# A list scheduler's clock model rewritten: durations by form of instruction, a port that VectorE and GpSimd share, and convolution taps put into VectorE's gaps

## The chip, the cores and the metric

The kernel runs on one core of a Trainium2 chip. The metric is the time of one execution on the device in microseconds; the time before is the median of three runs. A profile is one more execution of the same program, taken by the hardware profiler.

## The reference

One inference step of two layers, for a prompt of 1024 tokens and for 8 samples of 4 tokens each, which share the weights. The model width is 1024, everything is float32. Cut to what matters here:

```python
def even_layer(x, pos, conv_buf, kv_cache, pre_g, post_g, w_in, w_out, conv_w, conv_b, ln_g, ln_b):
    h = rms_norm(x, pre_g)
    proj = jnp.einsum('ntd,de->nte', h, w_in)                  # 1024 -> 7 * 1024
    a_val, a_gate, a_out_gate, qb, kb, vb, b_gate = jnp.split(proj, [...], axis=-1)
    ya, conv_new = conformer_conv(a_val, a_gate, conv_buf, conv_w, conv_b, ln_g, ln_b)
    ya = ya * jax.nn.silu(a_out_gate)       # GLU, causal depthwise conv of 31 taps, LayerNorm, swish
    q, k, v = rope(qb, pos), rope(kb, pos), vb                 # 16 heads of 64
    parts = [dswa_prompt(q, k, v, wnd, dil) for (wnd, dil) in ((128, 1), (512, 4), (2048, 16))]
    yb = dswa_merge(parts) * jax.nn.silu(b_gate)               # the samples use a cache of 2048 rows
    y = jnp.einsum('nte,ed->ntd', jnp.concatenate([ya, yb], axis=-1), w_out)
    return x + rms_norm(y, post_g), conv_new, k, v

def odd_layer(x, s0, lb, pre_g, post_g, w_in, w_out, g_norm):
    proj = jnp.einsum('ntd,de->nte', rms_norm(x, pre_g), w_in) # 1024 -> 4 * 2048
    qc, fc, ic, gate = jnp.split(proj, [...], axis=-1)
    o, s_new = hgrn2_recurrence(silu(qc), 1 - f, ic, log(f), s0)   # f = lb + (1 - lb) * sigmoid(fc)
    y = jnp.einsum('nte,ed->ntd', rms_norm(o, g_norm) * jax.nn.silu(gate), w_out)
    return x + rms_norm(y, post_g), s_new
```

## The kernel before

All instructions are recorded in one pass by a list scheduler that is part of the kernel. Every engine call goes through `Proxy` (its `g` is line 152, so nearly every row of the profile has that line), which emits the instruction and lets `account` (line 189) advance a model clock `clk` of that engine. The model clocks decide the order of emission; on the chip each engine runs its own instructions in that order and waits on semaphores where data is missing.

The dense work comes in **jobs** (`dense`, `plan_jobs`): 128 output channels of a projection, in three **chunks** of 384, 384 and 288 tokens. Weights and activations are split into a high and a low part, so a chunk is 24 matmuls of 128 rows by 128 columns (three for each of eight k-tiles) which sum in one PSUM bank: one of three banks named `d`, or one of four named `x` when `evacuate`'s queue is longer (`spare` in `dense`). The bank comes free when the job's `evac` has run, mostly a VectorE multiply out of PSUM (`b<-d`), for the rotary q and k also four ScalarE copies of 32 partitions each. `ahead` loads the next weights and splits them: ScalarE casts the high part, `w_split` subtracts it on VectorE or GpSimd, whichever clock is earlier, by a margin (128x1024 elements).

Everything else is **threads** of **atoms**, each with a kind (its engine), a priority and dependencies. After every third matmul of a chunk `sides` looks for an atom whose time has come: a TensorE atom if its data is in by the model 300 ns earlier (`LEAD`), another if it is ready and its engine's clock is at most so far ahead of TensorE's clock. So side work is put between the matmuls of the chunks. `tt` and `copy` choose the engine by the clocks too.

In layer 0 the jobs of a pair of heads come in the order ag, av, v, k, q, and there are eight pairs. Each pair brings two big threads:

- `attention`: for each of eight blocks of 128 queries a step `qk` (scores of two heads into two `x` banks, then on VectorE the mask and the maximum, on ScalarE the exponential), a step `tr` and from the third block on `far` (transposes of the probabilities, copied out of `x`), and a step `pv` (into bank `o`); `tr` of a block stands behind `qk` of the next. At the end `fin1` takes the reciprocal of the denominators on VectorE (128x16) and transposes it on TensorE.
- `conv_thread`: 25 taps on VectorE, each a `scalar_tensor_tensor` of 128x1024, behind one `tensor_scalar`, all in one accumulation; five more taps are made by ScalarE and GpSimd. Its priority number is 5, the last.

Layer 1 has 16 heads with four jobs each and a chunked recurrence; each layer ends with an output projection (`project`) whose last chunk runs through all 16 weights.

Of the kernel before, what the change touches and what calls it, by code (L numbers as in the profile page):

```python
# [12 lines left out]
OP = mybir.AluOpType  # L13
# [34 lines left out]
PTAPS = 5  # L48

# [13 lines left out]
class Arena:  # L63
    SIZE = {"page": 1056, "half": 520, "small": 136}
    BUFS = {"page": 28, "half": 17, "small": 5}
# [23 lines left out]
    def claim(self, o, need):  # L89
        """Sets what o may hold from now on, if that fits beside what the others hold or may still take."""  # L90
# [46 lines left out]
class Thread:  # L137
    def __init__(self, name, prio, atoms, dep=None, done=None):
        self.name, self.prio, self.atoms, self.pos = name, prio, atoms, 0
        self.dep, self.done, self.last = dep, done, 0.0  # L140
        self.owner = Owner()


class Proxy:
# [3 lines left out]
    def __getattr__(self, name):  # L148
        f = getattr(self.real, name)

        def g(*a, **k):
            r = f(*a, **k)  # L152
            self.kern.account(self.eng, name, a)
            return r
# [17 lines left out]
class Kern:  # L172
    def __init__(self, tc, io, arena, psum, dram):
# [5 lines left out]
        self.cur, self.eng, self.end = 0.0, None, 0.0  # L179
        self.xrel, self.drel, self.orel = [0.0] * NX, [0.0] * 3, [0.0]  # L180
# [8 lines left out]
    def account(self, e, name, a):  # L189
# [12 lines left out]
        ps = lambda i: len(a) > i and hasattr(a[i], "space") and a[i].space == bass.MemoryType.PSUM  # L202
        n = free_size(a[0]) if a and hasattr(a[0], "shape") else 0
        if len(a) > 1 and hasattr(a[1], "shape"):
            n = max(n, free_size(a[1])) if e != "pe" else n
        if name.startswith("preload"):
            d = 1283
        elif e == "pe":
            m = 32 if a[0].shape[0] <= 32 else 64 if a[0].shape[0] <= 64 else 128
            if name == "transpose":  # L210
                d = 109
            elif a[1].dtype == F32R:
                d = max(n / 2.4, 0.79 * m) + 3 if m == 128 else n / 2.4 * m / 128 + 25
            else:
                d = (2 * max(n / 1.2, 107) + 4 if m == 128 else n / 0.6 * m / 128 + 23 if m == 32 else
                     max(n / 1.2 + 36, 82))
        elif e == "dve":
            if name == "memset":
                d = 0.53 * n + 69
            elif name == "reciprocal":  # L220
                d = 6 * n + 69
            elif name == "tensor_scalar" and not ps(1):
                d = 0.52 * n + 160
            else:
# [2333 lines left out]
```

## Time and profile before

| | |
|---|---|
| three runs | 2482.09, 2483.13, 2484.84 us; median 2483.13 us |
| span of the profiled execution | 2483.4 us, from its first to its last instruction |
| TensorE busy | 2327.9 us (94%) |
| VectorE busy | 1698.1 us (68%) |
| ScalarE busy | 1080.3 us (44%) |
| GpSimd busy | 1034.0 us (42%) |
| mean granted TensorE clock | 0.971 of full speed |

The profiled execution's own time is its span; its difference to the median of the runs is 0.3 us. "Busy" is the time in which an engine had an instruction in work; for TensorE, whose matmuls overlap, it is not a measure of speed. In layer 0 VectorE is busy nearly all the time, in layer 1 TensorE is.

### The profile page before, as it was taken

How to read it: one execution, taken by the hardware profiler on the slowest of the kernel's cores; microseconds unless marked ns; L12 is line 12 of the kernel's file. 1: busy time of each engine (PE TensorE's matmuls, PEld its weight loads, DVE VectorE, ACT ScalarE, POOL GpSimd, SP SyncE). 2: the span in 40 equal slices, each digit the busy share in tenths (PEclk: the TensorE clock that was granted, in tenths of full speed). 3: DMA queues.
4: the chain of work that ended last, by engine and by line, in shares of the span. 5: the costliest groups of instructions: out<-in, count | busy, mean ns of one | idle time of the engine just before them, and what ended most of it. 6: DMA issues, size and time to landing. Idle time of an engine off the chain costs nothing.

```text
span 2483.4 us, 41427 instructions
## 1 busy us (share of the span) xinstructions
PE 2327.9 (94%) x16619; PEld 2173.2 (88%) x16619; DVE 1698.1 (68%) x2625; ACT 1080.3 (44%) x1972; POOL 1034.0 (42%) x670
## 2 busy tenths in 40 slices
PE   7899899988998989999979999999999999999997
PEld 6887887878878879889969999999999999999997
DVE  8888988978879765654395666666666556667437
ACT  5444535544545432334245444444444444444332
POOL 5553553643645443333262333333333333333334
PEclk9999999999999999999989999999999999999998
DMA  4121221312302687886252111111111221132525
GB/s 151 45 74 37 71 63 38 82 28 69 85 21 98 219 331 274 322 310 230 93 173 91 61 61 61 61 61 61 61 64 62 74 74 61 61 106 95 176 79 188
DMA packets 118168, 271.51 MB, mean 109 GB/s; under 512 B 32336, under 2 KB 59472, under 8 KB 117968
## 3 DMA queue, kind: packets, MB, share of 16 engines
q1 hardware_dynamic: 117968, 268.78, 31.7%
q8 instruction: 133, 2.18, 0.4%
q14 instruction: 67, 0.55, 0.1%
HBM read 215.00 MB, written 53.73 MB: 108 GB/s over the span
## 4 chain that ended last, share of the span: by engine, by line
PE 37%; DVE 14%; ACT 3%; issue 3%; DMA 1%; POOL 1%; SPq 0%; ACTq 0%; POOLq 0%; DVEq 0%
PE d L152 33%; DVE b L152 13%; PE x L152 4%; ACT b L152 3%; POOL b L152 1%; DVE c L152 1%; DMA b<-x1d 1%; DMA b<-vc 0%; DMA b<-woc 0%; POOL c L152 0%; ACT c L152 0%; SPq L152 0%; ACTq L152 0%; POOLq L152 0%; DVE b L2068 0%
## 5 line engine op out<-in xcount | busy, mean ns | idle before, releaser
L152 PE MATMUL d<-c,b 128*128 128x384 f32 (+1 forms) x10512 | 1845.9, 332 | 41.9 <-ACT b L152 29.9
L152 PEld LDWEIGHTS d<-c,b 128*128 128x128 f32 x10512 | 1730.1, 192 | 97.6 <-issue 44.3
L152 POOL TENSOR_TENSOR b<-b,b 128x1024 fp32r<-128x1024 f32 (+7 forms) x404 | 845.1, 2101 | 812.7 <-ACT b L152 557.8
L152 ACT ACTIVATE b<-b 128x384 f32<-128x384 f32 (+14 forms) x647 | 360.8, 567 | 887.8 <-DVE b L152 859.1
L152 DVE SCALAR_TENSOR_TENSOR b<-b,c,b 128x1024 f32<-128x1024 f32 (+2 forms) x258 | 399.4, 1550 | 24.6 <-ACT b L152 21.9
L152 DVE TENSOR_TENSOR b<-b,b 128x384 f32<-128x384 f32 (+15 forms) x411 | 351.2, 863 | 83.1 <-ACT b L152 66.0
L152 DVE TENSOR_TENSOR b<-d,b 128x384 f32<-128x384 f32 (+3 forms) x376 | 192.4, 513 | 281.9 <-PE d L152 280.6
L152 ACT CAST b<-b 128x1024 fp32r<-128x1024 f32 (+5 forms) x408 | 292.8, 724 | 43.8 <-DVE b L152 23.0
L152 PE MATMUL x<-b,b 128*32 128x128 f32 (+10 forms) x3712 | 289.1, 332 | 19.3 <-DVE b L152 13.6
L152 DVE SCALAR_TENSOR_TENSOR b<-b,b 128x384 f32<-128x384 f32 (+3 forms) x216 | 200.6, 933 | 114.6 <-ACT b L152 112.2
L152 PEld LDWEIGHTS x<-b,b 128*32 128x32 f32 (+2 forms) x3712 | 212.9, 138 | 73.4 <-issue 30.8
L152 PE MATMUL x<-c,b 128*128 128x128 f32 (+4 forms) x1024 | 153.5, 285 | 41.9 <-ACT b L152 25.4
L152 PEld LDWEIGHTS x<-c,b 128*128 128x128 f32 (+3 forms) x1024 | 124.4, 144 | 55.7 <-ACT b L152 30.6
L152 ACT COPY b<-d 32x384 f32<-32x384 f32 (+2 forms) x214 | 95.7, 447 | 136.3 <-DVE b L152 92.5
L152 POOL TENSOR_SCALAR b<-b 128x32 f32<-128x32 f32 x40 | 29.3, 733 | 294.0 <-DVE b L152 288.5
L152 DVE COPY b<-x 128x512 f32<-128x512 f32 (+5 forms) x239 | 110.6, 478 | 41.6 <-PE x L152 34.8
L152 POOL COPY b<-b 128x32 f32<-128x32 f32 (+1 forms) x105 | 59.9, 587 | 163.6 <-DVE b L152 161.4
L152 DVE CUSTOM_DVE_ANT_0 b<-x,b 128x256 f32<-128x256 f32 (+8 forms) x144 | 71.7, 535 | 76.3 <-PE x L152 76.3
L152 ACT COPY b<-x 128x512 f32<-128x512 f32 (+5 forms) x145 | 72.7, 512 | 112.7 <-PE x L152 110.1
L152 ACT ACTIVATE b<-b,c 128x512 f32<-128x512 f32 (+1 forms) x112 | 94.3, 872 | 1.9 <-DVE b L152 0.8
L152 POOL TENSOR_TENSOR b<-b,c 128x248 f32<-128x248 f32 (+1 forms) x48 | 59.3, 1252 | 72.1 <-ACT b L152 47.8
L152 DVE TENSOR_SCALAR b<-b,b 128x128 f32<-128x128 f32 x112 | 79.0, 705 | 4.0
(58 smaller groups left out, 926.9 us busy)
## 6 DMA issues: line engine op xcount, KB each, us to landing
b<-wc SPq DMA_DIRECT2D x64, 512.0 KB, 4.8
b<-wab SPq DMA_DIRECT2D x56, 512.0 KB, 5.6
b<-kc SPq DMA_DIRECT2D x64, 448.0 KB, 6.3
b<-vc SPq DMA_DIRECT2D x64, 448.0 KB, 8.0
b<-woa SPq DMA_DIRECT2D x32, 512.0 KB, 4.9
b<-woc SPq DMA_DIRECT2D x32, 512.0 KB, 4.4
b<-yd SPq DMA_DIRECT2D x16, 528.0 KB, 7.5
ybd<-b SPq DMA_DIRECT2D x16, 512.0 KB, 2.9
```

The source lines that it names most:

```text
L152: r = f(*a, **k)
```

## The change

`account` no longer has one formula for an engine: `array` (TensorE) follows the size of the array's part, its changes and the time at which a sum is really out; `cost` gives each form of VectorE, ScalarE and GpSimd instruction a duration, and says whether it needs the port that VectorE and GpSimd share; `share` then lengthens it by its overlap with the other engine's port time. Between engines a wait now costs `LAT` by engine instead of 140 ns, and an engine can begin its next instruction `OVER` earlier than its result is out. The other edits are rules: `fill`, called ahead of every VectorE instruction, emits ready VectorE atoms of priority above 4 (convolution taps) as long as the instruction would leave VectorE idle for over 700 ns; `sides` lets other engines run ahead of TensorE by 800 ns instead of 500; `evacuate` emits nothing for a sum that is not out yet by the model; `ahead` keeps to the number of pages it holds. The small buffers are 8 instead of 5, the half ones 512 instead of 520 columns. No arithmetic changes.

```diff
+QUEUE = 800
+HOLE = 700
+LAT = dict(pe=54.0, dve=33.0, act=33.0, pool=78.0)
+OVER = dict(dve=83.0, act=95.0, pool=54.0)
...
-    SIZE = {"page": 1056, "half": 520, "small": 136}
-    BUFS = {"page": 28, "half": 17, "small": 5}
+    SIZE = {"page": 1056, "half": 512, "small": 136}
+    BUFS = {"page": 28, "half": 17, "small": 8}
...
+        s = c[e] if self.eng == e else max(c[e], self.cur + LAT[e])
+        if e == "pe":
+            c[e], f = self.array(s, name, a, k)
+        else:
+            d, port = self.cost(e, name, a, k)
+            f = s + (self.share(e, s, d) if port else d)
+            c[e] = f - OVER[e]
+        self.cur, self.eng = f, e
+        self.end = max(self.end, f)
+    def fill(self, e):
+        if self.filling or e != "dve" or self.eng == e:
+            return
+        self.filling = True
+        start = self.cur + LAT[e]
+        while start - self.clk[e] > HOLE:
+            for t in self.threads:
+                r = None if t is self.running else self.ready(t)
+                if r is not None and t.atoms[t.pos].kind == e and t.prio > 4 and r <= self.clk[e] and self.fits(t):
+                    break
+            else:
+                break
+            old = self.cur, self.eng, self.end, self.taken
+            self.run_atom(t, r)
+            self.cur, self.eng, self.end, self.taken = old
+        self.filling = False
...
+        fast = name != "transpose" and a[1].dtype == F32R
+        if mode != self.mode:
+            s = max(s, self.done - 75)
+            self.mode, self.tiles = mode, {}
+            if mode == (128, 128):
+                s += 107
+        if mode == (128, 128):
+            d = max(0.4375 * n + 8, 107) if fast else 109 if name == "transpose" else 2 * max(0.8333 * n + 4, 111)
+            free, f = s + d, s + d + 165
...
+            ld = m / 1.2 + 20
+            one = max(0.4167 * n + 5 if fast else 0.8333 * n + 5, ld)
+            r = 1 if fast else 2
+            self.tiles[p] = s + r * one
+            free, f = s + 7 * r, s + ld + r * one + 165
+        self.done = max(self.done, f)
+        return free, f
...
+        if e == "act":
+            acc = "accum_out" in k
+            return n / 1.2 + (160 if psum else 200 if name == "activation" else 180) + 80 * ptr + 90 * acc, False
...
+            if k.get("op") == OP.mult:
+                return 1.75 * n + 100 if n >= 900 else 2.35 * n + 100, True
+            return 2.25 * n + 60, True
...
+        if name == "tensor_tensor_reduce":
+            return n / 0.96 + 237, two
+        if name == "scalar_tensor_tensor":
+            return n / 0.96 + (207 if ptr else 158), two
+        if name == "tensor_scalar":
+            if psum:
+                return n / 0.96 + (207 if ptr else 150), False
+            return (n / 1.92 + (280 if ptr else 150) if n >= 1024 else n / 0.96 + 153), True
+        if name == "tensor_copy":
+            return (n / 0.96 + 152, False) if psum else (n / 1.92 + 150, True)
+        return n / 0.96 + 150, two
...
+    def share(self, e, s, d):
+        other = self.port["pool" if e == "dve" else "dve"]
+        f, old = s + d, 0.0
+        while f > old:
+            old = f
+            f = s + d + sum(max(0.0, min(b, old) - max(a, s)) for a, b in other)
+        self.port[e] = [x for x in self.port[e] if x[1] > self.clk["pe"] - 5000] + [(s, f)]
+        return f - s
...
-            r = max(r, t.last)
+            r = max(r, t.last - (OVER[a.kind] + LAT[a.kind] if t.eng == a.kind and a.kind in OVER else 0.0))
...
-                    ok = r <= now + 300 and c[a.kind] <= now + 500 and (not a.bulk or c["dma"] <= now + 3000)
+                    ok = r <= max(now, c[a.kind]) + 60 and c[a.kind] <= now + QUEUE and (not a.bulk or c["dma"] <= now + 3000)
...
+        if best is None and self.pend:
+            n = len(self.pend)
+            self.clk["pe"] = max(self.clk["pe"], self.pend[0][4])
+            self.evacuate()
+            if len(self.pend) < n:
+                return
...
-            self.wown.claim["page"] = 5
+            self.wown.claim["page"] = max(5, min(self.wown.claim["page"], self.wown.held["page"]))
...
-                if n < d and V["t"] <= self.clk["pe"] + 200:
+                if n < d and V["t"] <= self.clk["pe"] + 200 and room(2):
                     self.w_high(V)
-            elif raws < min(d, RAWS):
+            elif raws < min(d, RAWS) and room(1):
...
         while self.pend:
             job, ch, o, taken, t, last = self.pend[0]
             if job.late is not None and not all(k in self.fin for k in job.late(ch)):
+                return
+            if t > max(self.clk["pe"], self.clk["dve"]) + 60:
                 return
```

`dense` hands `evacuate` the time `self.done` (the sum is out) instead of TensorE's clock, and `run` allows `fill` once the prologue is emitted. All other lines of the diff pass arguments or drop comments.

What the new numbers do to the order is seen in the programs. The count of instructions is the same on TensorE (15166 rows in each). First, VectorE in the fourth pair's attention, between the scores of the sixth block (128x416) and of the seventh (128x448). `ISA` is mask and maximum and the read of its accumulator, `COPY b<-x` takes transposes out of PSUM, `TENSOR_SCALAR` and `SCALAR_TENSOR_TENSOR` of 128x1024 with `c_87` are taps. Before:

```order
L152 ISA b_3931<-x,b_134 128x416
L152 ISA b_3931 128x1
L152 ISA b_3934<-x,b_134 128x416
L152 ISA b_3934 128x1
L152 SCALAR_TENSOR_TENSOR b_3628<-d,b_3628 128x256
L152 SCALAR_TENSOR_TENSOR b_3629<-d,b_3629 128x8x4
L152 COPY b_3962<-x 128x512
L152 COPY b_3980<-x 128x2x128
L152 TENSOR_SCALAR b_3987<-b_3628,c_87 128x1024
L152 SCALAR_TENSOR_TENSOR b_3987<-b_3628,c_87,b_3987 128x1024
L152 ISA b_4010<-x,b_134 128x448
```

and of the change:

```order
L157 ISA b_3959<-x,b_134 128x416
L157 ISA b_3959 128x1
L157 ISA b_3962<-x,b_134 128x416
L157 ISA b_3962 128x1
L157 COPY b_3992<-x 128x512
L157 SCALAR_TENSOR_TENSOR b_3272<-b_2669,c_87,b_3272 128x1024 x3
L157 ISA b_4015<-x,b_134 128x448
```

More taps stand between two softmax steps now. From the first softmax of a pair to its reciprocal there are 10 or 11 taps before in the second to the seventh pair, and 15 to 18 of the change; from the reciprocal to the next pair's first softmax 14 to 16 before, and 7 to 10 of the change.

Second, VectorE in the same pair's projections, at the job of k. `TENSOR_TENSOR b<-d` takes a chunk out of its bank. Before:

```order
L152 TENSOR_TENSOR b_3370<-d,b_132 128x384
L152 SCALAR_TENSOR_TENSOR b_3072<-b_2707,c_87,b_3072 128x1024 x2
L152 TENSOR_TENSOR b_3406<-d,b_132 128x384
L152 TENSOR_TENSOR b_3368<-b_3370,b_3369 128x384
L152 SCALAR_TENSOR_TENSOR b_3072<-b_2707,c_87,b_3072 128x1024 x2
L152 TENSOR_TENSOR b_3446<-d,b_132 128x288
```

and of the change:

```order
L157 TENSOR_TENSOR b_3344<-d,b_132 128x384
L157 SCALAR_TENSOR_TENSOR b_3272<-b_2669,c_87,b_3272 128x1024
L157 TENSOR_TENSOR b_3378<-d,b_132 128x384
L157 SCALAR_TENSOR_TENSOR b_3272<-b_2669,c_87,b_3272 128x1024
L157 TENSOR_TENSOR b_3414<-d,b_132 128x288
```

One tap stands between two chunks instead of two. On TensorE the chunks themselves move the other way: between a pair's first scores and the transpose of its denominators there are 141 matmuls of chunks before, and 75, 75, 105, 54, 87 and 87 of the change, in the second to the seventh pair; the 16 transposes of v move into that part, and stand directly ahead of the denominators. In the prologue the matmul that sums the squares of the first tokens stands 99th before and 148th of the change.

Third, VectorE in the last chunk of layer 0's output projection. `TENSOR_TENSOR` of 128x1024 is a weight's subtraction, `COPY b<-d` takes a sum out, `c_79<-` and `c_80<-` make layer 1's input. Before:

```order
L152 SCALAR_TENSOR_TENSOR b_10480<-b_10480,c_87,b_12063 128x384
L152 SCALAR_TENSOR_TENSOR b_10667<-b_10667,c_87,b_12063 128x384
L152 TENSOR_TENSOR b_12075<-b_12039,b_12074 128x1024
L152 SCALAR_TENSOR_TENSOR c_79<-b_10480,c_87,c_71 128x384
L152 TENSOR_TENSOR b_10818<-b_11746,b_10818 128x384
L152 COPY b_10480<-d 128x288
```

and of the change:

```order
L157 COPY b_10569<-d 128x288
L157 TENSOR_TENSOR b_12127<-b_12091,b_12126 128x1024
L157 SCALAR_TENSOR_TENSOR b_10791<-b_10791,c_87,b_12015 128x384
L157 TENSOR_TENSOR b_12158<-b_12118,b_12157 128x1024
L157 COPY b_10693<-d 128x288
```

From the first of these rows to the constants of layer 1 (`RECIPROCAL c`) VectorE has 4 subtractions of 128x1024 and 23 additions of 128x384 before, and 7 and 2 of the change; what it has no more stands later, or on GpSimd.

## Rows read from the trace of the kernel before

**Rows 1.** The page: its first line.

```profile
span 2483.4 us, 41427 instructions
```

**Rows 2.** Busy time by stage: each engine's us (instructions), granted clock, DMA.

```profile
core 0: us, PE busy (x) PEld busy (x) DVE busy (x) ACT busy (x) POOL busy (x), PEclk, DMA share, GB/s
62.00:860.00 798.00, 728.95 (x5425) 638.88 (x5424) 674.54 (x945) 378.90 (x824) 404.97 (x238) 0.94 0.23 68
860.00:1236.00 376.00, 365.35 (x3160) 331.58 (x3159) 197.06 (x366) 128.87 (x221) 138.71 (x115) 0.99 0.72 264
1236.00:1306.00 70.00, 51.75 (x322) 48.12 (x321) 63.93 (x68) 33.76 (x59) 40.82 (x19) 0.88 0.50 164
1306.00:2290.00 984.00, 965.18 (x6457) 945.64 (x6456) 614.28 (x1057) 445.08 (x717) 337.03 (x230) 1.00 0.21 70
```

**Rows 3.** The same columns within the fourth pair, cut three ways.

```profile
356.40:397.10 40.70, 39.04 (x236) 38.44 (x236) 38.52 (x37) 23.80 (x48) 24.54 (x15) 0.96 0.34 108
397.10:454.80 57.70, 51.34 (x425) 40.79 (x423) 44.98 (x82) 22.96 (x54) 25.18 (x16) 0.91 0.11 22
406.20:454.50 48.30, 44.95 (x385) 35.33 (x385) 36.90 (x71) 21.10 (x50) 22.26 (x13) 0.89 0.13 26
409.00:417.20 8.20, 7.67 (x43) 6.12 (x42) 4.99 (x12) 2.62 (x7) 3.19 (x1) 0.50 0.01 2
455.00:458.80 3.80, 3.80 (x19) 3.80 (x19) 3.46 (x2) 1.82 (x3) 3.80 (x3) 0.55 0.16 42
```

**Rows 4.** TensorE in order of time, fourth pair: start, us, what [idle before <-releaser].

```profile
386.95 4.48 PE L152 MATMUL d<-c,b 128*128 128x384 f32 x24 [1.46 <-ACT b L152]
407.07 0.79 PE L152 MATMUL x<-c,b 128*128 128x128 f32 x2 [2.74 <-ACT b L152]
454.84 0.27 PE L152 MATMUL x<-c,b 128*16 128x128 f32 x1 [1.99 <-DVE b L152]
```

**Rows 5.** VectorE in order of time, fourth pair: taps alone and beside GpSimd, the reciprocal.

```profile
384.88 1.27 DVE L152 SCALAR_TENSOR_TENSOR b<-b,c,b 128x1024 f32<-128x1024 f32 x1
448.22 5.84 DVE L152 SCALAR_TENSOR_TENSOR b<-b,c,b 128x1024 f32<-128x1024 f32 x3
```

**Rows 6.** Groups in 356.4:397.1 (three rows), then in 406.2:454.5, and VectorE's waits there.

```profile
L152 DVE SCALAR_TENSOR_TENSOR b<-b,c,b 128x1024 f32<-128x1024 f32 x15 | 25.9, 1729 | 0.2
L152 DVE TENSOR_TENSOR b<-d,b 128x384 f32<-128x384 f32 x4 | 2.2, 548 | 0.0
...
L152 PE MATMUL x<-c,b 128*128 128x128 f32 x12 | 1.5, 276 | 0.0
...
L152 DVE SCALAR_TENSOR_TENSOR b<-b,c,b 128x1024 f32<-128x1024 f32 x10 | 16.7, 1673 | 0.1
...
DVE b L152 <- PE x L152: 9.7, 8, 2.6
```

**Rows 7.** The chain that ended last, in order of time: start, us, matmuls of chunks.

```profile
2311.74 96.22 PE d L152 x552
2454.60 12.74 PE d L152 x94
```

**Rows 8.** TensorE in order of time, prologue.

```profile
39.38 1.65 PE L152 MATMUL x<-b,c 128*128 128x384 f32 x2 [2.80 <-DVE b L152]
```

**Rows 9.** 1236:1306: groups of VectorE, groups of GpSimd, and TensorE's waits.

```profile
L152 DVE TENSOR_TENSOR b<-b,b 128x384 f32<-128x384 f32 x23 | 22.0, 965 | 0.2
L152 DVE TENSOR_TENSOR b<-b,b 128x1024 fp32r<-128x1024 f32 x3 | 4.5, 1487 | 0.0
...
L152 POOL TENSOR_TENSOR b<-b,b 128x1024 fp32r<-128x1024 f32 x12 | 31.9, 2678 | 15.0 <-issue 10.2 <-ACT b L152 4.9
L152 POOL TENSOR_TENSOR b<-b,b 128x384 f32<-128x384 f32 x7 | 10.0, 1433 | 13.2 <-DVE b L152 9.7 <-ACT b L152 3.4
...
PE x L152 <- DVE b L152: 8.1, 2, 4.4
PE d L152 <- POOL b L152: 6.0, 5, 2.0
```

More of the change, by code (lines that the diff above doesn't have):

```diff
@@ L201, in account @@
             return
[L202 to L205, printed above, removed]
-        if name.startswith("preload"):
[L207 to L217, printed above, removed]
-            if name == "memset":
[L219 to L224, printed above, removed]
-                d = 1.042 * n + (130 if name == "scalar_tensor_tensor" else 70)
-        elif e == "act":
-            d = 0.833 * n + (51 if ps(1) else 94) + (93 if name == "activation" else 0)
-        else:
-            d = n * 2.1 + 150
@@ new lines, in cost @@
+    def cost(self, e, name, a, k):
+        aps = [x for x in list(a) + list(k.values()) if hasattr(x, "shape") and hasattr(x, "space")]
+        if name.startswith("preload"):
+            return 1283, False
+        n = max(free_size(x) for x in aps)
+        ins = [x for x in aps[1:] if not (free_size(x) == 1 and n > 1)]
+        ptr = len(ins) < len(aps) - 1
+        psum = any(x.space == bass.MemoryType.PSUM for x in ins)
+        two = sum(x.space != bass.MemoryType.PSUM for x in ins) > 1
+        if e == "act":
+            acc = "accum_out" in k
+            return n / 1.2 + (160 if psum else 200 if name == "activation" else 180) + 80 * ptr + 90 * acc, False
+        if e == "pool":
+            if name == "memset":
+                return 130 + 0.5 * n, False
+            if name == "tensor_copy":
+                return 170 + 0.9 * n, False
+            if name == "tensor_scalar":
+                return 250 + 1.1 * n, False
+            if k.get("op") == OP.mult:
+                return 1.75 * n + 100 if n >= 900 else 2.35 * n + 100, True
+            return 2.25 * n + 60, True
+        if name == "memset":
+            return 0.53 * n + 69, False
+        if name == "reciprocal":
+            return 6 * n + 130, False
+        if name == "tensor_reduce":
+            return n / 0.96 + 135, False
+        if name == "tensor_tensor_scan":
+            return 2 * n / 0.96 + 157, True
+        if name == "tensor_tensor_reduce":
+            return n / 0.96 + 237, two
+        if name == "scalar_tensor_tensor":
+            return n / 0.96 + (207 if ptr else 158), two
+        if name == "tensor_scalar":
+            if psum:
+                return n / 0.96 + (207 if ptr else 150), False
+            return (n / 1.92 + (280 if ptr else 150) if n >= 1024 else n / 0.96 + 153), True
+        if name == "tensor_copy":
+            return (n / 0.96 + 152, False) if psum else (n / 1.92 + 150, True)
+        return n / 0.96 + 150, two
@@ L503, in dense @@
                 if job.evac is not None:
-                    self.pend.append((job, ch, o, taken, c["pe"], n == len(job.chunks) - 1))
+                    self.pend.append((job, ch, o, taken, self.done, n == len(job.chunks) - 1))
                 elif n == len(job.chunks) - 1:
```

29 lines of the change are left out of this document (21 added, 8 removed).

## The prediction

> **What bounds the kernel now.** I read the stages first, then one pair of heads, then its waits, then the groups behind the waits. The profiled execution has a span of 2483.4 us [rows 1]; the median of the runs is 0.3 us less, so the sum is made against 2483.4 us. The stages [rows 2] show three kinds of work. From 62 to 860 us eight pairs of layer 0 pass: TensorE is busy 729.0 of 798.0 us at a granted clock of 0.94, VectorE 674.5, so that both are near their limit. From 860 to 1236 us, and in layer 1 (1306 to 2290 us), TensorE is busy 365.4 of 376.0 and 965.2 of 984.0 us at a clock of 0.99 and 1.00: there is little to win. From 1236 to 1306 us, between the layers, TensorE is busy only 51.8 of 70.0 us, VectorE 63.9.
>
> One pair stands for eight, since the same three waits come back in each. The fourth [rows 3] begins when the reciprocal of the pair before is out (356.4 us) and falls in two parts by TensorE's order: projections, 40.7 us, and from the first scores on (397.1 us) attention, 57.7 us; 98.4 us together. In it TensorE waits three times [rows 4]: 1.46 us for a bank, which ScalarE's copies free, behind VectorE's multiply; 2.74 us for the first softmax; 1.99 us for the reciprocal. Behind the second and the third the granted clock is lower: 0.50 for the 8.2 us from 409.0, 0.55 for the 3.8 us from 455.0 [rows 3], the lower of its two levels (1.2 GHz), after waits of two to three microseconds. The reciprocal is late because three taps stand ahead of it on VectorE, 5.84 us from 448.22 on [rows 5]. Meanwhile VectorE itself is idle for 11.4 of the 48.3 us from the first softmax to the reciprocal [rows 3], 9.7 us of that in eight waits for scores or transposes of TensorE [rows 6]. So one engine waits where the other has too much queued, and changes places with it later in the pair.
>
> **The change, part by part.** *Taps go from the projections into the attention.* By the order, 7 taps fewer stand in the projections of a pair in the middle, and 6 more in the attention. Their price is the same in both parts, 1.73 and 1.67 us [rows 6]. Three evacuations of 0.55 us [rows 6] and about one subtraction of 1.49 us [rows 9] come to the projections. VectorE has there 38.5 - 12.1 + 1.6 + 1.5 = 29.5 us of work. In the attention it has 36.9 + 6.2 x 1.67 - 1.6 = 45.7 us: the 10.4 us of taps fit the 11.4 us of idle time nearly to the microsecond.
>
> *Chunk matmuls go the other way.* The second to seventh pairs have 80.5 of them in the attention in the mean, where 141 stood: 60.5 fewer. 552 matmuls of 384 columns took 96.22 us, 94 mostly of 288 took 12.74 us [rows 7], so 0.174 and 0.136 us each, 0.161 in the mix of two to one: 9.7 us. The 16 transposes of v go from the projections into the attention, 2.0 us (12 took 1.5 us [rows 6]). TensorE has in the projections 39.0 + 9.7 - 2.0, less 1.6 us for the low clock (0.96 of 40.7 us), 45.1 us of work, with VectorE's 29.5 as cover for every evacuation: I take 46, as the bank is not late any more. In the attention it has 51.3 - 9.7 + 2.0 = 43.6 us, 39.5 if the 8.2 us at half clock go.
>
> *Sum of a pair.* Projections are then bound by TensorE (46) and the attention by VectorE (45.7, say 46): 92 us is the lower bound if a tap keeps its price. The upper one is a backlog: before, 9.1 us pass from the first scores (397.1) to the first softmax (406.2), because VectorE is still at work for the projections; if all of that stayed, 101 us. With 16 us of slack ahead of it I let a quarter stay: 94.3 us, 4.1 less than 98.4. The waits agree with that: if those for the bank and the reciprocal went with the low clock behind the latter, 1.46 + 1.99 + 1.7 = 5.2 us would come back; the wait for the first softmax I keep, for a tap still stands directly ahead of it. Seven pairs (the second to the eighth): 29 us. Bounds: 7 x 2.6 = 18 us lost, and 73 us gained if taps got cheap (third rival).
>
> A rule of the Trainium skill speaks against cheap taps. A tap alone takes 1.27 us, three beside GpSimd's additions take 5.84 / 3 = 1.95 each [rows 5]. The Trainium skill (SBUF — State Buffer, Who interferes with whom) says that a VectorE instruction with two inputs in SBUF and a GpSimd instruction that reads SBUF take a shared port in turn, for the whole instruction. By that rule a tap pays the same wherever it stands, as long as GpSimd has the same work; the trace agrees (1.73 and 1.67 us). The sum by it is the 94.3 us above, and at 1.27 us a tap it would be 88.
>
> *Prologue.* The sum of squares waits 2.80 us for VectorE [rows 8] and stands 48 matmuls later now, 7.7 us at 0.161: that wait goes, 3 us. Less than nothing is not in sight, since the matmuls ahead of it need none of it.
>
> *Between the layers.* VectorE is the bound (63.9 of 70.0 us). Ahead of layer 1's constants it now has 21 additions fewer (0.97 us each, 20 us) and 3 subtractions more (1.49, 4.5 us) [rows 9]; GpSimd does additions for 1.43 us each, and loses subtractions of 2.68. TensorE's 6.0 us of waits for GpSimd [rows 9] should go; the 8.1 us behind VectorE are for the sums of squares, which need all additions, wherever they are made, and I keep them. So 6 us gained; bounds: 15 us (VectorE's whole relief), and 5 us lost if what stands later now holds up layer 1's first chunk.
>
> *The rest at nothing.* In layer 1 chunks alternate between `d` and `x` banks now. TensorE's idle time there is 18.8 of 984 us [rows 2]; no wait of the list above lives there. If banks of `x` ran short, recurrence steps would wait: 10 us either way for the range. Page limits in `ahead` cost nothing as long as weights land before their job; none of the three waits of [rows 4] is ended by a DMA.
>
> Sum: 2483.4 - 29 - 3 - 6 = **2445 us**.
>
> **Rivals.** *Slower: the attention starves TensorE and its clock falls.* With ten chunk matmuls a step (1.6 us) instead of 18, and two or three taps between two softmax steps, TensorE may wait in each of eight steps. For it speaks that a wait of 2.74 us was followed by 8.2 us at 0.50; against it that the wait of 1.46 us was not, and that 6 us a pair of such waits shared over eight steps are under 1 us each. Price: each microsecond at half clock adds 0.5 to TensorE's 39.5 us. It passes VectorE's 46 at 13 us of half clock in an attention, and the pair is slower than before (over 52.4 us) from 26 us on. At 31 us it is 55 + 46 = 101 us: 2.6 x 7 = 18 us lost, with the two other terms about **2492 us**.
>
> *The pair keeps its length.* VectorE's 83.5 us and TensorE's 90.4 us of busy time in 98.4 do not shrink by order, only the waits do; if half of the backlog stays and the first softmax comes later than now, a pair takes 97.5: 6 + 9 us, **2468 us**. For it: the added taps stand ahead of the scores' maximum in a fixed order.
>
> *Taps get cheap.* If GpSimd's work moves under TensorE-bound stretches, taps at 1.27 us bring the attention to 45.7 - 16.7 x 0.4 = 39 us; TensorE's 39.5 to 43.6 then bound it, and a pair takes 88: 73 + 9 us, **2401 us**. Rows 6 speak against it.
>
> *The change doesn't do what it says.* The model may plan the same waits to other places, so that gains and losses cancel: within 0.2% (5 us, about what a measurement of this kernel can tell from no change) of **2483 us**.
>
> **How the numbers follow.** I give the forecast 0.47, the pair that keeps its length 0.17, cheap taps 0.10, no change 0.10, the starved TensorE 0.16. Faster by over 0.2% are the first three, 0.74; the same 0.10; slower 0.16. The time is the forecast's, 2445 us. Half of the cheap taps' chance lies under 2404 us and half of the slower case over 2490 us; that leaves out 0.13, and the bounds of the pair (94.3 down to 92, up to 97.5) and of the part between the layers lie within.
>
> **What would show it.** A pair of about 94 us; taps of 16 or more between first softmax and reciprocal with VectorE idle for less than 4 us there; no wait over 1.5 us for a `d` bank behind ScalarE; a smaller wait for the reciprocal; a granted clock above 0.94 in layer 0; from the output projection's last chunk to layer 1 about 64 us instead of 70; layer 1 unchanged. It is wrong if TensorE's waits in the attention add up to more than the projections gain, if the half-clock stretches become longer than 26 us a pair, or if VectorE's first softmax still comes 9 us after the scores.

## The result, and the profile after

The changed kernel takes 2396.69 us (median of four runs, 2392.17 to 2401.23) beside 2482.61 us for the kernel before on the same chip: ratio 0.9647, 95% interval 0.963 to 0.9664. The forecast was 2445 us, range 2404 to 2490 us: the direction was right, the gain of 86 us is more than twice the 38 us forecast. The profiled execution spans 2399.4 us [rows 1: 2483.4], by the page's first line:

```profile
span 2399.4 us, 41471 instructions
```

The gain is cut at landmarks that are the same in both programs: the reciprocals of the pairs, the last chunk of layer 0's output projection (its first and last matmul), and the scans of layer 1's heads on VectorE. Starts are read from the timelines.

| from, to | before | after | difference | forecast |
|---|---|---|---|---|
| start, first reciprocal | 163.3 | 153.9 | -9.4 | -3 |
| first, seventh reciprocal (six pairs) | 584.9 | 546.5 | -38.4 | -24.6 |
| seventh reciprocal, last chunk of the output projection | 487.6 | 479.2 | -8.3 | -4.1 |
| that chunk | 76.5 | 52.5 | -24.0 | } -6 |
| its end, second scan | 85.0 | 95.1 | +10.1 | } |
| second, sixteenth scan (14 heads) | 830.7 | 810.3 | -20.4 | 0 |
| sixteenth scan, end | 255.4 | 261.9 | +6.5 | 0 |

In the third row lies the eighth pair. It takes 106.9 us, 98.1 before, but 510 matmuls of chunks lie in it instead of 375; the stretch behind it, to the last chunk, is 17.1 us shorter.

The busy times in the columns of [rows 2]: first the six pairs and the last chunk of the output projection in the kernel before, then the six pairs, the last chunk and the 14 heads of the changed kernel, then its fourth pair's two parts, from reciprocal to first softmax and from there to the next reciprocal.

```profile
163.30:748.20 584.90, 534.27 (x3936) 468.36 (x3936) 498.85 (x699) 280.62 (x612) 301.32 (x176) 0.94 0.20 58
1235.75:1312.28 76.53, 58.28 (x370) 54.57 (x369) 67.63 (x71) 36.00 (x61) 43.93 (x21) 0.89 0.51 169
...
153.90:700.40 546.50, 507.59 (x3954) 450.02 (x3954) 505.34 (x688) 281.46 (x616) 261.21 (x164) 0.99 0.21 61
1179.65:1232.14 52.49, 52.17 (x388) 51.43 (x388) 47.43 (x39) 26.49 (x40) 41.77 (x20) 1.00 0.65 207
1327.30:2137.60 810.30, 807.42 (x5500) 796.73 (x5500) 506.67 (x862) 374.54 (x596) 285.99 (x185) 1.00 0.19 66
335.00:382.30 47.30, 44.74 (x273) 44.04 (x273) 39.72 (x44) 28.26 (x56) 36.63 (x24) 0.99 0.26 82
382.30:427.20 44.90, 41.37 (x386) 32.23 (x386) 41.00 (x72) 16.60 (x43) 5.30 (x4) 0.93 0.13 29
```

The granted clock in the six pairs is 0.99, before 0.94: an estimate from the two rows is that (1 - 0.94) x 584.9 = 35 us of full-speed TensorE time were not granted before, and 5 us are not in the changed kernel. VectorE's busy time in the six pairs did not fall (498.85 and 505.34 us). The fifth busy time, GpSimd's, is what the forecast had not moved: 36.63 us beside the projections and 5.30 us beside the attention, where 24.54 and 22.26 us stand in [rows 3]; cut by the same landmarks, the six pairs have 28.4 and 21.9 us in the mean before, 36.5 and 7.1 us after. The groups of VectorE's taps in the same two parts, and its waits in the second:

```profile
L157 DVE SCALAR_TENSOR_TENSOR b<-b,c,b 128x1024 f32<-128x1024 f32 x8 | 14.3, 1787 | 0.1
...
L157 DVE SCALAR_TENSOR_TENSOR b<-b,c,b 128x1024 f32<-128x1024 f32 x18 | 25.2, 1400 | 0.2
```

```profile
DVE b L157 <- PE x L157: 3.5, 2, 3.3
```

18 taps in the attention cost 1.40 us each, not 1.67; 8 in the projections 1.79 [rows 6: 1.73 and 1.67]. In the mean of the six pairs 16.3 taps in the attention cost 1.39 us and 8.0 in the projections 2.05 us; before, 9.5 cost 1.65 and 15.7 cost 1.73 us. So the contention has not gone: it stands beside the projections now, where TensorE is the limit. VectorE waits 3.5 us instead of 9.7 [rows 6]. TensorE in order of time, fourth pair, answers to [rows 4]; the wait for a `d` bank behind ScalarE is gone, that for the softmax (3.02 us) and that for the reciprocal (1.85 us) are not:

```profile
383.14 0.86 PE L157 MATMUL x<-c,b 128*128 128x128 f32 x2 [3.02 <-ACT b L157]
...
427.73 0.27 PE L157 MATMUL x<-c,b 128*16 128x128 f32 x1 [1.85 <-DVE b L157]
```

Behind the output projection's last chunk there are two new long waits, for the sums of squares of layer 1's norm:

```profile
1243.61 2.61 PE L157 MATMUL x<-b,c 128*128 128x384 f32 x4 [9.35 <-DVE b L157]
...
1266.95 1.65 PE L157 MATMUL x<-b,c 128*128 128x384 f32 x2 [7.03 <-DVE b L157]
```

### The profile page after: what moved, and what is told of

Its sections match the earlier page's. It is cut to its first block, busy times and chain, and to the rows that moved or that the text cites. A ratio compares the mean times of both kernels' runs of the same rounds, so it can differ in the third digit from the quotient of the medians.

```text
span 2399.4 us, 41471 instructions
## 1 busy us (share of the span) xinstructions
PE 2277.0 (95%) x16619; PEld 2141.0 (89%) x16619; DVE 1700.2 (71%) x2567; ACT 1094.7 (46%) x2000; POOL 1047.6 (44%) x700
## 4 chain that ended last, share of the span: by engine, by line
PE 70%; DVE 18%; ACT 3%; issue 3%; DMA 3%; POOL 2%; SPq 0%; DVEq 0%; ACTq 0%; POOLq 0%
PE d L157 41%; PE x L157 29%; DVE b L157 18%; ACT b L157 3%; POOL b L157 2%; DMA b<-vc 1%; PE o L157 1%; DVE c L157 1%; DMA b<-x 1%; DMA b<-kc 0%; DMA ybd<-b 0%; DMA b<-rd 0%; SPq L157 0%; DMA b<-x1d 0%; DMA cpo<-b 0%
## 5 line engine op out<-in xcount | busy, mean ns | idle before, releaser
L157 PE MATMUL d<-c,b 128*128 128x384 f32 (+1 forms) x8064 | 1410.7, 330 | 18.3 <-ACT b L157 7.8
L157 PEld LDWEIGHTS d<-c,b 128*128 128x128 f32 x8064 | 1317.7, 190 | 49.8 <-issue 23.1
L157 POOL TENSOR_TENSOR b<-b,b 128x1024 f32<-128x1024 f32 (+8 forms) x418 | 834.2, 2007 | 833.7 <-ACT b L157 600.7
L157 PE MATMUL x<-c,b 128*128 128x384 f32 (+4 forms) x3472 | 560.1, 311 | 30.1 <-DVE b L157 16.3
L157 PEld LDWEIGHTS x<-c,b 128*128 128x128 f32 (+2 forms) x3472 | 514.0, 174 | 57.8 <-ACT b L157 22.5
L157 PE MATMUL x<-b,b 128*32 128x128 f32 (+11 forms) x3760 | 295.7, 329 | 6.2 <-POOL b L157 2.3
L157 DVE TENSOR_TENSOR b<-x,b 128x288 f32<-128x288 f32 (+3 forms) x157 | 79.6, 507 | 127.9 <-PE x L157 112.9
L157 DVE COPY b<-x 128x512 f32<-128x512 f32 (+6 forms) x214 | 96.0, 463 | 59.9 <-PE x L157 53.6
L157 POOL COPY b<-b 128x32 f32<-128x32 f32 (+2 forms) x105 | 56.4, 546 | 152.4 <-DVE b L157 150.2
L157 PE MATMUL o<-b,b 128*64 128x128 f32 (+1 forms) x864 | 59.7, 269 | 27.4 <-DVE b L157 26.1
```

## The experiments

My theory after the result: **GpSimd's long instructions hold up VectorE less where something waits for VectorE** (in the pairs because they moved under TensorE-bound projections, in layer 1 because fewer of them stand beside short VectorE instructions that TensorE waits for), and the port in the model does that. The rivals: the place of the taps alone (by `fill` or by the new durations), or the new rules. Below, "pair" is the mean of the second to seventh pair from reciprocal to reciprocal, "head" the mean from the second to the sixteenth scan, ratios are to the kernel before on the same chip, with 95% intervals.

| run | us | ratio | pair | head |
|---|---|---|---|---|
| before | 2482.61 | | 97.5 | 59.3 |
| after | 2396.69 | 0.963 to 0.9664 | 91.1 | 57.9 |
| e1_no_fill | 2410.68 | 0.9689 to 0.9735 | 91.8 | 57.8 |
| e2_no_port | 2601.36 | 1.0456 to 1.0506 | 108.8 | 59.6 |
| e3_old_rules | 2391.7 | 0.9617 to 0.9662 | 89.6 | 57.8 |
| e4_old_durations | 2475.81 | 0.9964 to 0.9988 | 98.6 | 58.5 |
| e5_short_adds_before | 2451.48 | 0.9855 to 0.9895 | 93.9 | 59.3 |
| e6_short_adds_after | 2379.4 | 0.9564 to 0.9603 | 88.5 | 57.9 |
| e7_pieces_before | 2437.78 | 0.9802 to 0.9843 | 96.0 | 57.9 |
| e8_old_rules_lag | 2398.23 | 0.9637 to 0.9675 | 90.0 | 57.8 |
| e9_port_alone | 2520.88 | 1.0134 to 1.0168 | 99.3 | 57.8 |
| e10_pieces_old_rules | 2381.62 | 0.9573 to 0.9605 | 89.7 | 57.7 |
| e11_pieces_after | 2386.41 | 0.9582 to 0.9617 | 90.4 | 57.8 |
| e12_pieces_in_model | 2405.91 | 0.9659 to 0.9704 | 91.9 | 57.4 |
| e13_old_tensor | 2488.75 | 1.0011 to 1.0041 | 94.9 | 57.6 |
| e14_slow_taps | 2399.62 | 0.9646 to 0.9704 | 89.9 | 57.8 |

**Which part of the change does it.** Four kernels each take one part out of the changed one.

```diff
# e1_no_fill
-HOLE = 700
+HOLE = 1e9
# e2_no_port (share)
+        return d
         other = self.port["pool" if e == "dve" else "dve"]
# e3_old_rules (sides, evacuate, dense)
-ok = r <= max(now, c[a.kind]) + 60 and c[a.kind] <= now + QUEUE and ...
+ok = r <= now + 300 and c[a.kind] <= now + 500 and ...
-            if t > max(self.clk["pe"], self.clk["dve"]) + 60:
-                return
-self.pend.append((job, ch, o, taken, self.done, ...
+self.pend.append((job, ch, o, taken, c["pe"], ...
# e4_old_durations: account's old formulas for all engines, 140 ns between engines
```

> The changed kernel without fill (its threshold HOLE is set out of reach), all else as changed. Theory A, taps put into VectorE's gaps by fill make the pairs shorter: a pair (reciprocal to reciprocal) goes from 91 us back towards 98, 2425 to 2440 us in all. Rival B, the new durations and rules already place the taps: a pair stays below 93 us, 2392 to 2405 us in all.

> The changed kernel whose model has no shared port: share returns the bare duration, so VectorE and GpSimd do not lengthen each other in the model. Theory A, the port in the model keeps GpSimd's long additions away from short VectorE instructions that TensorE waits for: layer 1's waits of 0.7 us come back, a head takes 59 us instead of 57.5, and a pair loses 2 us or more, 2425 to 2440 us in all. Rival B, the plain durations are enough: a head stays at 57.5 us, 2392 to 2405 us in all.

> The changed kernel with the old rules of sides (ready up to 300 ns ahead, engines at most 500 ns ahead of TensorE) and of evacuate (a sum is taken as soon as its last matmul is issued by the model). Theory A, the rules let side work run where it does not make TensorE wait: waits for the softmax and the reciprocal come back, a pair takes 95 us or more, 2420 us or more in all. Rival B, the durations decide: a pair at 91 to 92 us, 2390 to 2405 us in all.

> The changed kernel with the old durations and the old 140 ns between engines, all new rules kept (fill, queue of 800 ns, page limits). Theory A, the new durations carry the gain: a pair takes 96 us or more, a head of layer 1 takes 59 us, 2455 us or more in all. Rival B, the rules carry it: 2390 to 2420 us.

`fill` is worth 14 us, little of it in the pairs (91.8 beside 91.1 us): theory A of that run fell, though the time lies above rival B's range. The eighth reciprocal comes at 806.7 us without `fill` and at 807.3 us with it, but 17 of the 200 taps are then still to be done, with `fill` none; the second scan comes at 1340.6 and 1327.3 us. The rules of `sides` and `evacuate` are worth nothing: with the old ones the kernel is 5 us faster, about what can be told from no change. The old durations with all new rules give nearly all of the gain back (2475.81 us, theory A). By stages e4 says more: its pairs are 1.1 us longer than before, and the output projection's last chunk takes some 80 us, about as long as before, where e3's takes 52.6 us; so both gains come with the durations. But from the seventh reciprocal to the second scan e4 takes 632.3 us, where the kernel before takes 649.1 and the changed one 626.8: most of that stretch's gain needs no new duration, and which of the parts that e4 keeps (`fill`, the other rules, the page limits, the buffers) brings it stays open. `LAT` and `OVER` were only taken out together with the durations. And the new durations without the port are 120 us slower than before (2481.29 us on that chip), far outside the ranges of both theories. The fourth pair there, its projections and its attention by windows, and the wait for its reciprocal in TensorE's timeline:

```profile
385.10:446.00 60.90, 46.91 (x265) 44.72 (x265) 55.25 (x56) 27.07 (x54) 30.90 (x19) 0.86 0.25 81
446.00:495.40 49.40, 43.90 (x394) 34.27 (x394) 29.95 (x62) 19.82 (x49) 19.69 (x11) 0.95 0.10 15
```

```profile
495.79 0.37 PE L157 MATMUL x<-c,b 128*16 128x128 f32 x1 [4.88 <-DVE b L157]
```

A model that counts a tap at 1.27 us wherever it stands has VectorE idle when on the chip it is not. It puts 18 taps into the projections, and VectorE's 55.25 us of work bound them. My detail on layer 1 was wrong there: heads take 59.6 us, but by waits for ScalarE (15 of them, 21.0 us in all), not by the old ones.

**What the contention costs.** Two pairs of kernels keep the order of instructions and change only what GpSimd does. The model counts the instructions in full in all of them.

```diff
# e5_short_adds_before, e6_short_adds_after (conv_thread, padd)
-                nc.gpsimd.tensor_tensor(z, z, t.f, op=OP.add)
+                nc.gpsimd.real.tensor_tensor(z[:, :8], z[:, :8], t[:, :8], op=OP.add)
+                self.account("pool", "tensor_tensor", (z, z, t.f))
# e7_pieces_before, e11_pieces_after; e10 has e3's rules too (w_split)
+                for n in range(4):
+                    ns = slice(256 * n, 256 * n + 256)
+                    self.nc.gpsimd.real.tensor_tensor(lo.r[:, ns], raw[:, ns], hi[:, ns], op=OP.subtract)
+                self.account("pool", "tensor_tensor", (lo.r, raw.f, hi.f))
```

> The kernel before in its own order of instructions, but GpSimd's additions for the convolution (128x512, 10 halves of products of which 8 are added per pair, 1.9 us each) touch only 8 columns on the chip; the model still counts them in full. So most columns of the convolution lack four of its 31 taps. Theory A, the changed order gains because it takes GpSimd's port time out of the stretch where VectorE is the limit: here that time disappears in the old order, a tap falls from 1.7 towards 1.4 us and a pair from 98 to 94 us or less, 2435 to 2455 us in all. Rival B, the place of the taps alone matters: a pair stays above 96.5 us, 2468 to 2482 us in all.

> The same cut in the changed kernel, in its own order of instructions: GpSimd's additions for the convolution touch only 8 columns on the chip, the model counts them in full. Theory A, those additions now lie beside TensorE-bound projections: the pair stays at 90 to 91.5 us, 2385 to 2397 us in all, so that the distance to the kernel before shrinks. Rival B, contention costs the same in both orders: this kernel falls by as much as the kernel before does under the same cut, the distance stays at 80 us or more.

> The kernel before in its own order, but each of GpSimd's weight subtractions (128x1024, 2.4 us) is made in four pieces of 256 columns, counted as one by the model. Theory A, VectorE and GpSimd take the port in turn by whole instructions: in layer 1 the 128x128 scaling that stands beside a subtraction takes 0.9 us or less instead of 2.4, TensorE's wait of 0.7 us behind it goes, a head takes 58.3 us or less instead of 59.1, 2455 to 2470 us in all. Rival B, the small instruction waits until GpSimd is through anyway: it keeps its 2.4 us and a head its 59.1 us, 2475 to 2490 us in all.

> The changed kernel with the old rules of sides and evacuate, in that order of instructions, and GpSimd's weight subtractions made in four pieces of 256 columns (counted as one by the model). In the kernel before the pieces took 47 us off. Theory A, the new order avoids what the pieces cure in layer 1, but not in layer 0: a pair falls by 1 to 2 us, the part between the layers by some us, the heads by nothing, 2370 to 2383 us in all. Rival B, the new order has cured all of it: 2388 to 2395 us in all.

> The changed kernel as it is, with GpSimd's weight subtractions in four pieces (counted as one by the model). Theory A: 12 to 25 us less, 2372 to 2385 us in all, none of it in the heads of layer 1, which stay at 57.5 us. Rival B, nothing left to cure: 2392 to 2400 us in all.

Without the additions the old order is 33 us faster (2484.85 to 2451.48 us): theory A of e5, with a pair of 93.9 us and taps of 1.43 us in the attention. The changed order is 17 us faster (2396.69 to 2379.4; 16 by the ratios, as the two were taken beside different runs of the kernel before): half, and neither theory of e6. The heads don't move, as the convolution is layer 0's: a control. Short additions also end earlier for everything that waits for GpSimd, so 33 and 17 us are at most what the port costs there. With the subtractions in four pieces the old order is 47 us faster, more than theory A of e7 gave, and the heads fall from 59.3 to 57.9 us, 20.8 us in the 14 heads, as much as by the change. The changed order is only 10 us faster (12 by the ratios), just short of theory A of e11, its heads nothing. With e3's rules (e10) the pieces take 10 us off as well, 2391.7 to 2381.62 us, in theory A's range, but the pair that should have fallen by 1 to 2 us stays (89.6 and 89.7 us): no single stage gives more than 2.2 us. In the old order a head's wait is seen in three rows, VectorE, GpSimd and TensorE in the timeline. Behind them stand groups over the 14 heads: VectorE's scaling before, after and in e7, GpSimd's pieces in e7; and last TensorE's waits for VectorE in the heads, before and after (us in total, times, longest):

```profile
1621.36 2.40 DVE L152 TENSOR_SCALAR b<-b,b 128x128 f32<-128x128 f32 x1
...
1621.33 2.35 POOL L152 TENSOR_TENSOR b<-b,b 128x1024 fp32r<-128x1024 f32 x1 [3.23 <-ACT b L152]
...
1623.82 0.82 PE L152 MATMUL x<-b,b 128*128 128x128 f32 x3 [0.46 <-DVE b L152]
```

```profile
L152 DVE TENSOR_SCALAR b<-b,b 128x128 f32<-128x128 f32 x98 | 69.0, 704 | 3.5
...
L157 DVE TENSOR_SCALAR b<-b,b 128x128 f32<-128x128 f32 x99 | 52.2, 528 | 3.5
...
L152 DVE TENSOR_SCALAR b<-b,b 128x128 f32<-128x128 f32 x98 | 39.5, 403 | 3.5
...
L424 POOL TENSOR_TENSOR b<-b,b 128x256 fp32r<-128x256 f32 x172 | 122.3, 742 | 47.4 <-ACT b L152 47.1
...
PE x L152 <- DVE b L152: 13.2, 29, 1.1
...
PE x L157 <- DVE b L157: 2.9, 2, 1.9
```

An instruction that takes 0.29 us alone (at 1620.72 us, say) begins 0.03 us behind GpSimd's and ends 0.08 us behind it, after 2.40 us. The mean of this scaling over the heads is 704 ns before, 528 ns after, 403 ns with the pieces, and TensorE's waits behind VectorE there are 13.2, 2.9 and 0 us. The Trainium skill (SBUF — State Buffer, Who interferes with whom) says of a VectorE instruction in a 2-port mode, which tensor_scalar can enter, that whichever of it and GpSimd's issues first has the shared port for the whole instruction and the other blocks; the three rows agree with that, and no run shows in which mode the scaling ran. The mean alone does not give a head's time: in e2 it is 401 ns, and heads take 59.6 us.

**Is the port enough, and which clocks must be right.**

```diff
# e9_port_alone (before, with cost and share only for the overlap, and ahead's page limits)
+        if e in self.port and self.cost(e, name, a, k)[1]:
+            d = self.share(e, s, d)
# e13_old_tensor (after)
-            c[e], f = self.array(s, name, a, k)
+            # d by the old formula
+            c[e] = f = self.done = s + d
# e14_slow_taps (after, cost of scalar_tensor_tensor)
-            return n / 0.96 + (207 if ptr else 158), two
+            return (n / 0.96 + (207 if ptr else 158)) * (1.2 if ptr and n == 1024 else 1), two
```

> The kernel before with one part of the change alone: in its model, VectorE and GpSimd instructions with two inputs in SBUF lengthen each other by their overlap (share). All durations, the 140 ns between engines and the rules stay old, apart from the page limits of ahead. Theory A, the port in the model is what moves GpSimd's work out of the attention and taps into it: a pair takes 93 us or less and a head of layer 1 57.5 us, 2400 to 2430 us in all. Rival B, the port helps only beside right durations: a pair stays above 96 us, 2450 to 2490 us in all.

> The changed kernel with TensorE's old formula in account (array unused; a sum is out when its last matmul is issued), all else as changed. Theory A, the durations of VectorE and GpSimd with their port carry the gain and TensorE's formula does not matter: 2385 to 2410 us in all, heads of layer 1 at 57.5 us. Rival B, TensorE's formula is needed, since all other clocks are measured against TensorE's: VectorE then looks late or early beside it, taps pile up, 2425 us or more.

> The changed kernel whose model takes 20% more for a tap alone (1.53 us instead of 1.27), all else as changed. Theory A, a VectorE that is counted too slow leaves taps behind, as with the port on old durations: by the order 14 of 200 taps are left when the eighth pair's reciprocal is out, where the change leaves none; the second to seventh pair get shorter than 91 us and what is left is paid later, 2385 to 2400 us if VectorE's idle time behind the pairs takes it, 2405 us or more if it must be done at once. Rival B, an error of that size doesn't show: the pairs take 91 us as before, 2392 to 2402 us.

Neither theory of e9 holds: at 2520.88 us it is slower than the kernel before and outside both ranges. In layer 1 the port is enough: heads at 57.8 us, the scaling at 287 ns. In layer 0 three pairs take 92.2, 89.1 and 81.7 us with 18, 17 and 18 taps where 25 fall due, and the next takes 124.8 us with 34. What is owed is then paid at once, as VectorE's and TensorE's timelines show:

```profile
481.30 13.16 DVE L152 SCALAR_TENSOR_TENSOR b<-b,c,b 128x1024 f32<-128x1024 f32 x10
...
496.48 1.09 PE L152 MATMUL x<-b,b 128*128 128x256 f32 x3 [12.64 <-DVE b L152]
```

The six pairs together lose only 11 us to the kernel before. The larger loss of e9 lies behind them: from the eighth reciprocal to the second scan it takes 593.5 us, where the kernel before takes 551.0. 25 taps are still to be done there, the last at 1015 us. The convolution's stores (`yad`) come after them, from 1091.5 us on instead of 962.7, and in SyncE's order the loads of the samples' cached keys (`kc`) stand between these stores. TensorE's and SyncE's timelines:

```profile
1148.02 2.89 PE L152 MATMUL x<-b,b 128*32 128x512 f32 x3 [51.11 <-DMA b<-kc]
...
1143.24 0.32 SPq L152 DMA_DIRECT2D yad<-b  x1
1143.61 2.33 SPq L152 DMA_DIRECT2D b<-kc  x4
```

A second wait there, 33.92 us up to 1308.27 us, is for GpSimd's additions ahead of a sum of squares.

e9 and e13 have in common the port and TensorE's old formula, which counts a chunk matmul of 384 columns at 163 ns; 552 of them took 174 ns each [rows 7]. So by the model VectorE is late beside TensorE, and its taps are left behind. That the formula does it is shown for e13, which changes nothing else; for e9 it is argued, since it keeps all other old durations too (a tap counts 1.20 us there, less than the 1.27 us that it takes alone). e13 leaves taps behind in the same way: 19 to 21 in the second to fifth pair, 29 in the sixth, which takes 107.7 us, and 19 are left behind the eighth reciprocal. Its time is rival B's, but of its 84 us over the changed kernel 47 lie behind that reciprocal, with a wait of 28.44 us for the same loads. A fifth more on a tap alone (e14) does no harm: the pairs take 89.9 us, 14 taps are left behind the eighth reciprocal, and VectorE has room for them there, theory A.

**Two tries at more.** e8 lets TensorE's sums of squares between the layers wait (on e3); e12 lets the model count the pieces (on e3).

```diff
# e8_old_rules_lag (post, ready)
+            atoms[-1].lag = 12000 if c < 2 else 0
-        return r
+        return r + getattr(a, "lag", 0)
# e12_pieces_in_model: as e10, but by self.nc.gpsimd.tensor_tensor, so each piece is counted
```

> The changed kernel with the old rules of sides and evacuate, and the two matmuls between the layers that sum squares for layer 1's norm (chunks 0 and 1) are taken to be ready 12 us later by the model. There TensorE stood for 18.5 us behind VectorE. Theory A, TensorE only stands in a wrong place in its order: it does the first chunks of layer 1 meanwhile, 8 to 18 us less than with the old rules alone, 2374 to 2384 us in all. Rival B, VectorE's additions bound this part and the sums of layer 1's chunks can't leave their banks before: the wait only moves, 2388 to 2395 us in all.

> The changed kernel with the old rules of sides and evacuate and GpSimd's weight subtractions in four pieces that the model counts one by one (636 ns each, 2.5 us together). Theory A, a model that knows the pieces gains as much as the pieces alone or more: 2360 to 2380 us in all. Rival B, four counted pieces make GpSimd look late, more subtractions go to VectorE, and the gain is lost: 2388 us or more.

TensorE's waits from the eighth reciprocal to the second scan, in e3 and then in e8 (us in total, times, longest):

```profile
PE x L157 <- DVE b L157: 22.1, 4, 18.5
...
PE d L157 <- DVE c L157: 2.0, 1, 2.0
```

```profile
PE d L157 <- DVE c L157: 18.2, 7, 4.6
PE x L157 <- DVE b L157: 10.4, 4, 6.8
```

The wait for the sums is shorter in e8, and another takes its place, for the parts of layer 1's input that VectorE makes (`c`): VectorE bounds this stretch, the mechanism of rival B, and e8 is even some us above that rival's range. e12 ends in rival B's range, but not for its reason: VectorE makes 32 of the subtractions in e3 and in e12. TensorE stands there once for 26.3 us, from 1178.7 us on, until GpSimd's additions are out that a sum of squares needs. The best kernel that leaves nothing out is e10, 2381.62 us (ratio to before 0.9573 to 0.9605).

## Why the prediction was right and wrong

**The pairs (-4.1 us forecast, -6.4 measured).** The two-part picture held: in the mean of the six pairs 45.6 us pass from the reciprocal to the first scores and 3.4 us from there to the first softmax (46 and a backlog of 2.3 were forecast), 16 or more taps stand in four of the six attentions (14 to 18), VectorE is idle there for less than 4 us, and TensorE has no wait for a `d` bank. The attention takes 42.1 us, where 45.7 were forecast. **The step that failed** is "By that rule a tap pays the same wherever it stands, as long as GpSimd has the same work": GpSimd did not have the same work. 1.39 us instead of 1.65 for each of 16.3 taps in the mean of the six pairs are 4.2 us of VectorE's time in the attention. I had ordered VectorE and TensorE and left GpSimd where it was, though its order had changed as well; "Rows 6 speak against it" used a price measured beside GpSimd's old place. The third rival had the mechanism (GpSimd's work moves under TensorE-bound stretches), but with bare taps at 1.27 us and a pair of 88 us it went too far: 1.39 us and 91.1 us. That the time, 2396.69 us, lies next to that rival's 2401 is luck in part, as the rival had nothing from layer 1.

How much of the pair's gain is less contention: with the short additions the two orders differ by 93.9 - 88.5 = 5.4 us instead of 6.4, with the pieces by 96.0 - 90.4 = 5.6. So 1.0 and 0.8 of the 6.4 us; what is left, 4.6 us, is near the 4.1 that waits and places of taps were to give. That the two shares add up is argued, no kernel has both cuts. The clock is part of that rest: the 35 and 5 us that were not granted (an estimate, above) differ by some 30 of the six pairs' 38 us, while TensorE's waits there fell only from 50.6 to 39.5 us in all, the longest from 4.3 to 3.0 us. No run changes the clock alone, so its share is not shown.

**Prologue (-3, measured -9.4).** The wait of 2.80 us [rows 8] is gone. What I left out is the clock behind it. The same window of both kernels, columns as in [rows 2], before and then after:

```profile
38.90:45.70 6.80, 6.02 (x15) 4.65 (x16) 3.57 (x5) 3.13 (x5) 4.32 (x7) 0.50 0.00 1
```

```profile
38.90:45.70 6.80, 5.46 (x30) 4.12 (x29) 1.70 (x3) 2.97 (x6) 2.58 (x4) 1.00 0.01 1
```

6.8 us at 1.2 GHz did half of what they could, 3.4 us; the rest, some 3 us, was not traced.

**Between the layers (-6, measured -24.0 + 10.1 = -13.9).** The sum's sign was right, and it lies within the bound of 15 us; the parts were not forecast. In the last chunk TensorE's waits for GpSimd's subtractions went as forecast, and its waits for VectorE inside it as well: TensorE is busy for 52.17 of 52.49 us at a clock of 1.00, before 58.28 of 76.53 us at 0.89. The step that failed is "I keep them": the sums of squares, kept at 8.1 us [rows 9], now stand behind the chunk and wait 9.35 and 7.03 us. In e8, which has e3's rules, a later place for them only moved the wait.

**Layer 1 (0 forecast, measured -20.4 in 14 heads, +6.5 behind them).** "no wait of the list above lives there" was the failing step, with a larger miss than the six pairs (20.4 beside 13.8 us): I had listed waits above 1.4 us, and 29 waits of at most 1.1 us, 13.2 us in all, lie in the 14 heads. e7 shows the cause, short VectorE instructions held up by a whole subtraction (20.8 us less in the heads without any change of order), and the scaling is the one that the rows show ahead of TensorE's wait; e9 shows that the port in the model alone moves it away. The loss at the end has a wait of 4.21 us for a GpSimd subtraction at 2174.68 us; the rest of it stays open.

**The whole.** Of the 48 us that the forecast missed, some 14 lie in the six pairs, 4 in the stretch behind them, 14 in layer 1 (20 in the heads, less what is lost at the end), 8 between the layers and 6 in the prologue. With the additions short and with the subtractions in pieces the kernel before gets 33.4 and 47.1 us faster, the changed one 17.3 and 10.3. The differences are 16 and 37 us; that they add up, and that they are the missing time, is argued. Of the rivals, the starved TensorE came only in small: ahead of the attention's `pv` it waits for VectorE 21 times in the six pairs, 20.4 us in all, never over 1.7 us (before 5.3 us), and the clock there is 0.99; the half-clock stretches that the rival needed did not come. That the model may plan the same waits to other places was true of the change with one part taken out (e4, e13), not of the whole.

## What to carry to other kernels

When a scheduler's numbers change, read the order of every engine, also of the one that nobody waits for: a price taken beside another engine's work holds only while that work stands there. In this list scheduler the clocks had to be right against each other: each of three partial corrections (no port, port alone, old TensorE) left the kernel no better than before or slower, while a fifth too much on one form (e14) cost nothing. Work that a wrong clock leaves behind can hold up more than its own engine: in e9 and e13 loads stood behind late stores in one queue, and TensorE waited 51 and 28 us. Where a short instruction of one engine is held up by a long one of another, cut the long instructions of the engine with time to spare: four pieces took 47 us off the old kernel, without any change of order, and 10 us off the changed one.

## What the hardware showed unexpectedly

The pieces cost GpSimd time (4 x 0.742 = 2.97 us instead of 2.38 for a subtraction), and the kernel still gains, since VectorE's short instructions get their turn between them. Of TensorE's waits in the changed kernel's fourth and fifth pair, that of 3.02 us (up to 383.14 us) goes with a granted clock of 0.50, the lower of its two levels, from 381.70 to 388.50 us; behind those of 1.85 and 1.55 us the granted clock is 1.00.
